# Two blocks on one core: the low halves of all weight chunks are subtracted on VectorE

## The chip, the cores and the metric

The program runs on one core of one Trainium2 chip. The metric is the device time of one execution in microseconds (us), the median over several runs. PE is TensorE's matmul part, PEld its weight load, DVE is VectorE, ACT is ScalarE, POOL is GpSimd, SP is SyncE, which here only issues DMAs.

## The reference, cut to what matters

The reference runs two transformer-like blocks over 512 tokens of width 1024, in fp32. The first has a recurrent branch (a short convolution and a gated linear recurrence) beside an attention branch; the second has a pooling branch, a differential attention branch over 512 latent and 256 context tokens, an RWKV branch (a recurrent state that is run forward and backward), a gated merge of the three, and a mixture of 32 experts. What touches the change are the large projections:

```
proj = einsum('bsd,de->bse', h, w_in[l])            # first block, 3072 columns
mix  = einsum('bse,ed->bsd', concat([ya, yb]), w_out[l])
p_l  = modulate(x, norm1_g, ...) @ w_in[l]          # second block, 7040 columns
p_c  = modulate(ctx, norm1_g, ...) @ w_in[l]        # the context's 256 tokens
merged = sum_n sigmoid(gates_n) * (branches[n] @ w_br[n]);  mix_l = merged @ w_out[l]
```

## The kernel before, in words

The tile framework assigns no engine: each instruction is written for one. Its planner then places all instructions of an engine in one order, by simulated costs of its own, and each engine executes its instructions strictly in that order; semaphores make them wait for one another.

Every projection is made with about fp32 accuracy out of three matmuls in a faster format (`mm3`, L307 to L312). For that each operand is split into a high part, which is the value rounded to that format, and a low part, which is the rest. The weights come from DRAM in chunks of 128 partitions x 1024 values (512 KB). `load_chunk` (L293) issues the DMA on SP, and `split_chunk` (L299) makes the two halves: ACT copies `raw` into `hi` (tile names `wr` and `wh` in the profile), and then `lo = raw - hi` (`wl`) is a TENSOR_TENSOR of 128x1024. Its engine is `cur.get("lo", GP)`: POOL, unless `cur["lo"]` has been set. There are 125 chunks. The first 50 belong to the first block and the context's projections, 53 to the RWKV stage of the second block (from L1089, where `cur["lo"] = V` is set, to L1520, where it is taken away), and 22 to what comes after: a few that the planner places beside the last RWKV batches, the three branch merges (`merge`, L1550) and the output projection (L1795).

The stages in order of time, in the traced execution: the first block's q, k, v projections, its attention, and its recurrent projections (0 to about 345 us, POOL makes `lo`); the first output projection and the context's projections, beside which the first block's result is normed (to 485 us, POOL); the RWKV stage (to about 1133 us, DVE); differential attention with the merges in between, and the output projection (to about 1440 us, POOL); the experts (to the end), whose weights are not split.

Names that the steps below touch: `rope` (L551; POOL makes `o = src*cos` at L554, DVE `a` at L556 and `o + a` at L559); `conv` (L931; `xa`); `tok_ss` (L1013; sums of squares, `sbs` on DVE at L1020, `sbp` on PE); `gate_b` (L1028; `yb` on POOL at L1032); `qk_norm` and L901 (the context's keys, `kc`); `rsq` (L320; a DVE step, then a power on POOL at L323, as in `rm`, `kcnr`, `h2r`); the scaling of the first block's result `mix` (L1070, L1073) and its norm (L426); `shift` (L724; tiles `al`, `kt`, `vt`, and a tile also called `wl`, L727 and L728, which is not the low half of weights); `scores` of the differential attention (L1652; `dpl` on PE, a maximum on DVE, `P` on ACT).

PE writes a projection's result into one of three PSUM buffers of the tag `mm`; a chunk's first matmul waits until the buffer that it takes has been read out.

Of the kernel before, what the change touches and what calls it, by code (L numbers as in the profile page):

```python
# [9 lines left out]
F32 = mybir.dt.float32  # L10
# [3 lines left out]
ALU = mybir.AluOpType  # L14
# [171 lines left out]
def build(tc, A, out, dbg=None, upto=99):  # L186
    with ExitStack() as ctx:
        _build(ctx, tc, A, out, dbg, upto)


def _build(ctx, tc, A, out, dbg, upto):
    nc = tc.nc
    V, SC, GP, PE, SY = nc.vector, nc.scalar, nc.gpsimd, nc.tensor, nc.sync
# [5 lines left out]
    cur = {}  # L199

    def weights(name, bufs, side, raw=None):

        if cur.get("wctx"):
            cur["wctx"].close()
            cur["wctx"] = None
        if bufs:
            cur["wctx"] = ctx.enter_context(ExitStack())
            cur["wp"] = cur["wctx"].enter_context(tc.tile_pool(name=name, bufs=1, side=side, reuse_waits="tile"))
            cur["wb"] = bufs
            cur["wraw"] = raw or bufs  # L210
# [3 lines left out]
    def subpool(name, nb):  # L214

        if cur.get("sub"):
            cur["sub"].close()
            cur["sub"] = None
        if nb is None:
            return  # L220
        cur["sub"] = ctx.enter_context(ExitStack())
        cur["bp"] = cur["sub"].enter_context(tc.tile_pool(name=name, bufs=1, reuse_waits="tile"))
        NB.clear()
        NB.update(nb)
# [17 lines left out]
    def psum(name, bufs):  # L242

        if "pctx" in cur:
            cur["pctx"].close()
        cur["pctx"] = ctx.enter_context(ExitStack())
        cur["pp"] = cur["pctx"].enter_context(tc.tile_pool(name=name, bufs=1, space=PSUM, reuse_waits="tile"))
        PB.clear()
        PB.update(bufs)
# [43 lines left out]
    def load_chunk(w, c0, kt=8, name="w", nw=128, k0=0, kn=2):  # L293

        raw = cur["wp"].tile([128, kt, nw], F32, tag="raw", name=name + "r", bufs=cur["wraw"])
        n = c0 // 128 if nw == 128 else c0 // 256 * kn + k0 // 4
        cur["ld"] = SY.dma_start(raw.rearrange("p k n -> p (k n)"), w[n]).ins
        return raw

    def split_chunk(raw, name="w"):  # L300
        kt, nw = raw.shape[1], raw.shape[2]
        hi = cur["wp"].tile([128, kt, nw], F32R, tag="hi", name=name + "h", bufs=cur["wb"])
        lo = cur["wp"].tile([128, kt, nw], F32R, tag="lo", name=name + "l", bufs=cur["wb"])
        SC.activation(hi, raw, AF.Copy)  # L304
        cur.get("lo", GP).tensor_tensor(lo, raw, hi.bitcast(F32), ALU.subtract)  # L305
        return hi, lo

    def mm3(p, ah, al, bh, bl, start, stop):
# [42 lines left out]
    def step(n=1):  # L351

        while n and fill:
            try:
                next(fill[0])
                n -= 1
            except StopIteration:
                fill.pop(0)
# [158 lines left out]
    def halves(w, c0):  # L517

        return [split_chunk(load_chunk(w, c0, kt=4, nw=256, k0=4 * kh)) for kh in range(2)]
# [566 lines left out]
    weights(None, 0, None)  # L1086
    cp2 = wctx.enter_context(tc.tile_pool(name="c2", bufs=1, side="right", reuse_waits="tile"))
    weights("wp1", 3, "right", 2)
    cur["lo"] = V  # L1089
    psum("pp2", {"mm": (2, 512), "aux": (3, 512), "ch": (1, 512), "pa": (2, 512)})  # L1090
    scope("b2a", {})
    rp = cur["bp"]
# [425 lines left out]

    gate(24 - GL - ngate[0])
    step(99)  # L1520
    cur.pop("lo")
    subpool(None, None)


# [264 lines left out]
    for c in range(4):  # L1789
        po2 = [ps("po2", "aux" if c % 2 else "mm") for _ in range(2)]  # L1790
        for kh in range(2):
            hi, lo = split_chunk(load_chunk(A["w_out_2"], 256 * c, kt=4, nw=256, k0=4 * kh))
# [339 lines left out]
```

## Time and profile before

| | us |
|---|---|
| runs shown | 1940.88, 1953.85, 1959.17 |
| median | 1953.85 |
| the profiled execution's own time | 1948.57 |
| its span, first to last instruction | 1946.8 |

| engine | busy us | share of the span |
|---|---|---|
| PE | 1732.8 | 89% |
| DVE | 1062.6 | 55% |
| ACT | 618.2 | 32% |
| POOL | 406.4 | 21% |

Of POOL's 406.4 us the 72 subtractions of weight chunks are 181.3. The mean granted TensorE clock is 0.938 of full speed, and it switches between two levels, 1.2 and 2.4 GHz. Busy time is that of instructions from start to end; an instruction of DVE or POOL that cannot go on is counted as busy too.

### The profile page before, as it was taken

The page shows a single profiled execution, that of the slowest core. Times are in us where ns is not written, and L with a number is a line of the kernel's source. Part 1 is how long each engine was busy: PE and PEld are TensorE (multiplying, and loading weights), DVE is VectorE, ACT ScalarE, POOL GpSimd, SP SyncE. Part 2 cuts the span into 40 slices and gives each one's busy share as a digit, 9 for nine tenths or more (in the row PEclk, how much of TensorE's full clock was granted, in tenths as well). Part 3 has the DMA queues.
Part 4 walks back from the last instruction along what each step waited for, and adds up shares of the span by engine and source line. Part 5 has one row for each costly group of instructions (what it writes and reads, how often), then busy time and mean ns, then how long its engine had stood idle before and what let it go on. Part 6 is the DMA issues. An engine that isn't in the chain of part 4 may idle for free.

```text
span 1946.8 us, 31337 instructions
## 1 busy us (share of the span) xinstructions
PE 1732.8 (89%) x12309; PEld 1233.5 (63%) x12310; DVE 1062.6 (55%) x2417; ACT 618.2 (32%) x1164; POOL 406.4 (21%) x326
## 2 busy tenths in 40 slices
PE   6899997966888988978889986989979999999998
PEld 3874567963565777767768864777944545444544
DVE  4555686174479845767777744676342333332432
ACT  4224454453444232333333333443221111110110
POOL 2520337351004101111220013722211010100000
PEclk8999998988988997889989998989989999999999
DMA  8335622567647545445565346635449999999998
GB/s 294 108 112 207 215 76 90 171 217 223 173 128 194 148 141 115 138 93 142 140 147 144 108 160 210 234 122 177 186 165 386 386 386 386 386 387 387 386 386 288
DMA packets 275296, 415.90 MB, mean 214 GB/s; under 512 B 104876, under 2 KB 126408, under 8 KB 274888
## 3 DMA queue, kind: packets, MB, share of 16 engines
q1 hardware_dynamic: 246248, 383.44, 59.4%
q10 hardware_dynamic: 25568, 16.78, 2.8%
q0 software_dynamic: 3328, 13.63, 2.5%
q8 instruction: 98, 1.61, 0.3%
q14 instruction: 54, 0.44, 0.1%
HBM read 370.26 MB, written 43.53 MB: 213 GB/s over the span
## 4 chain that ended last, share of the span: by engine, by line
PE 43%; DVE 5%; DMA 5%; ACT 1%; issue 1%; SPq 0%; POOL 0%; ACTq 0%; DVEq 0%; POOLq 0%
PE ped L1976 6%; PE peg L1937 6%; PE peu L1944 6%; PE pcb L2008 3%; PE po L1799 2%; PE pg L1910 2%; DMA kb<-kbD 2%; PE pg L1911 2%; PE pW L1283 1%; PE pf L312 1%; PE pf L310 1%; PE pf L311 1%; PE pbr L310 1%; PE pbr L311 1%; PE pbr L312 1%; PE dpo L1683 1%
## 5 line engine op out<-in xcount | busy, mean ns | idle before, releaser
L305 POOL TENSOR_TENSOR wl<-wr,wh 128x1024 fp32r<-128x1024 f32 x72 | 181.3, 2528 | 306.6 <-ACT wh L304 300.2
L304 ACT ACTIVATE wh<-wr 128x1024 fp32r<-128x1024 f32 x125 | 131.7, 1055 | 172.7 <-PE pf L311 61.0
L310 PE MATMUL pf<-h2h,wh 128*128 128x512 f32 x344 | 144.5, 420 | 20.7 <-ACT mth L1348 14.4
L311 PE MATMUL pf<-h2l,wh 128*128 128x512 f32 x344 | 142.6, 415 | 0.0
L312 PE MATMUL pf<-h2h,wl 128*128 128x512 f32 x344 | 141.8, 412 | 0.0
L1982 POOL TENSOR_TENSOR yl<-ey,yh 128x512 fp32r<-128x512 f32 x30 | 38.4, 1280 | 464.6 <-ACT yh L1981 464.6
L1976 PE MATMUL ped<-wd,hid 128*64 128x512 f32 (+1 forms) x528 | 127.4, 585 | 0.7 <-ACT hid L1960 0.7
L1937 PE MATMUL peg<-wg,hTg 128*64 128x512 f32 x512 | 127.0, 597 | 0.0
L1944 PE MATMUL peu<-wu,hTg 128*64 128x512 f32 x512 | 125.2, 595 | 0.0
L1195 DVE TENSOR_TENSOR Tm<-LT,Ti 128x60 f32<-128x60 f32 (+24 forms) x372 | 87.5, 235 | 43.2 <-DMA LT<-atD 35.0
L2009 DVE TENSOR_TENSOR acc<-acc,pcb 128x512 f32<-128x512 f32 (+1 forms) x124 | 76.0, 665 | 49.1 <-PE pcb L2008 49.0
L310 PEld LDWEIGHTS pf<-h2h,wh 128*128 128x128 f32 x344 | 67.5, 196 | 40.7 <-ACT mth L1348 14.7
L1197 DVE TENSOR_TENSOR Ti<-Ti,Tm 128x60 f32<-128x60 f32 (+24 forms) x372 | 82.4, 221 | 8.4
L1976 PEld LDWEIGHTS ped<-wd,hid 128*64 128x64 f32 x528 | 39.6, 136 | 70.9 <-issue 67.1
L1944 PEld LDWEIGHTS peu<-wu,hTg 128*64 128x64 f32 x512 | 42.9, 137 | 65.4 <-issue 64.1
L305 DVE TENSOR_TENSOR wl<-wr,wh 128x1024 fp32r<-128x1024 f32 x53 | 65.1, 1228 | 32.3 <-ACT wh L304 32.0
L1937 PEld LDWEIGHTS peg<-wg,hTg 128*64 128x64 f32 x512 | 41.9, 137 | 60.9 <-issue 58.4
L311 PEld LDWEIGHTS pf<-h2l,wh 128*128 128x128 f32 x344 | 67.6, 196 | 18.1 <-issue 3.2
L312 PEld LDWEIGHTS pf<-h2h,wl 128*128 128x128 f32 x344 | 67.2, 195 | 17.4 <-issue 1.1
L1981 ACT ACTIVATE yh<-ey 128x512 fp32r<-128x512 f32 x30 | 18.9, 630 | 163.5 <-DVE ey L1980 90.0
L1914 ACT ACTIVATE hTg<-pg,sh,gs 128x128 f32<-128x128 f32 x64 | 28.2, 457 | 121.4 <-PE peu L1944 55.4
L1917 DVE TENSOR_SCALAR hTg<-pg,gs,sh 128x128 f32<-128x128 f32 x64 | 25.3, 408 | 75.0 <-PE peu L1944 38.4
(962 smaller groups left out, 4468.0 us busy)
## 6 DMA issues: line engine op xcount, KB each, us to landing
wg<-in_w_exp_gate_dram SPq DMA_DIRECT2D x64, 1024.0 KB
wu<-in_w_exp_up_dram SPq DMA_DIRECT2D x64, 1024.0 KB
wd<-in_w_exp_down_dram SPq DMA_DIRECT2D x62, 1024.0 KB
wr<-in_w_in_dram SPq DMA_DIRECT2D x97, 512.0 KB
kb<-kbD SPq DMA_DIRECT2D x24, 384.0 KB
wr<-in_w_out_dram SPq DMA_DIRECT2D x16, 512.0 KB
LT<-atD SPq DMA_DIRECT2D x12, 512.0 KB
thD<-mth ACTq DMA_DIRECT2D x24, 256.0 KB
```

The costliest lines, as they stand in the source:

```text
L304: SC.activation(hi, raw, AF.Copy)
L305: cur.get("lo", GP).tensor_tensor(lo, raw, hi.bitcast(F32), ALU.subtract)
L310: PE.matmul(p, ah, bh, start=start, stop=False)
L311: PE.matmul(p, ah, bl, start=False, stop=False)
L312: PE.matmul(p, al, bh, start=False, stop=stop)
L1195: V.tensor_tensor(tmp[:, :nj, :n], bc(LT[:, s, None, ts_], [128, nj, n]), bc(T[:, js, s:s + 1], [128, nj, n]), ALU.mult)
L1197: V.tensor_tensor(T[:, js, ts_], T[:, js, ts_], tmp[:, :nj, :n], ALU.add)
L1937: mm = PE.matmul(pg[64 * a:64 * a + 64, :], hT[:, k, 64 * a:64 * a + 64], gp[a][k // 4][:, k % 4, :], start=(k == 0), stop=(k == 7), tile_ ...
L1944: PE.matmul(pu[64 * a:64 * a + 64, :], hT[:, k, 64 * a:64 * a + 64], up[a][k // 4][:, k % 4, :], start=(k == 0), stop=(k == 7), tile_posit ...
L1976: PE.matmul(pd[64 * a:64 * a + 64, :], hid[:, m * k + 64 * a:m * k + 64 * a + 64], dn[q][a][:, k, 0:q1 - q0], start=(k == 0), stop=(k == 3 ...
L2008: PE.matmul(p, ohT[R, 128 * i:128 * (i + 1)], yy[R, qs], start=(z == 0), stop=(z == len(parts) - 1))
L2009: V.tensor_tensor(acc[i][:, qs], acc[i][:, qs], p, ALU.add)
```

## The change

`split_chunk` subtracts on VectorE always, and the two lines that switched the engine around the RWKV stage are gone.

```diff
@@ split_chunk
         SC.activation(hi, raw, AF.Copy)
-        cur.get("lo", GP).tensor_tensor(lo, raw, hi.bitcast(F32), ALU.subtract)
+        V.tensor_tensor(lo, raw, hi.bitcast(F32), ALU.subtract)
         return hi, lo
@@ before the RWKV stage
     weights("wp1", 3, "right", 2)
-    cur["lo"] = V
@@ after it
     step(99)
-    cur.pop("lo")
     subpool(None, None)
```

The planner makes a new order from it. All 125 subtractions stand on DVE, and none on POOL. The order of the first half of the RWKV stage is what it was; in its second half chunks and batches are interleaved otherwise.

On POOL, around the gating of the first block's attention branch, before (`yb` is the gated branch, `sar`, `sbr` and `kcnr` are powers in `rsq`):

```order
L305 TENSOR_TENSOR wl<-wr,wh 128x1024 x14
L1032 TENSOR_TENSOR yb_1457<-yb_1457,gbth 128x512
L305 TENSOR_TENSOR wl<-wr,wh 128x1024
L1032 TENSOR_TENSOR yb_1672<-yb_1672,gbth 128x512
L323 TENSOR_TENSOR sar<-sar,cst_75 128x4
L305 TENSOR_TENSOR wl<-wr,wh 128x1024
L1032 TENSOR_TENSOR yb_1911<-yb_1911,gbth 128x512
L305 TENSOR_TENSOR wl<-wr,wh 128x1024
L1032 TENSOR_TENSOR yb_2101<-yb_2101,gbth 128x512
L305 TENSOR_TENSOR wl<-wr,wh 128x1024 x2
L323 TENSOR_TENSOR sbr<-sbr,cst_75 128x4
```

and on POOL at the same place now:

```order
L1032 TENSOR_TENSOR yb_1457<-yb_1457,gbth 128x512
L1032 TENSOR_TENSOR yb_1672<-yb_1672,gbth 128x512
L1032 TENSOR_TENSOR yb_1911<-yb_1911,gbth 128x512
L323 TENSOR_TENSOR sar<-sar,cst_75 128x4
L1032 TENSOR_TENSOR yb_2101<-yb_2101,gbth 128x512
L323 TENSOR_TENSOR sbr<-sbr,cst_75 128x4
L323 TENSOR_TENSOR kcnr<-kcnr,cst_75 128x8 x2
```

Nothing stands between the gating steps any more.

On DVE, at the rotary embedding of q (`qra` and `qro` are `a` and `o` of `rope`, `xc` is the context), before:

```order
L556 TENSOR_TENSOR qra<-q_377,SIN 128x512
L426 TENSOR_SCALAR xc_2127<-xc_2127,hcr 128x1024
L426 TENSOR_SCALAR xc_2129<-xc_2129,hcr 128x1024
L556 TENSOR_TENSOR qra<-q_378,SIN 128x512
L559 TENSOR_TENSOR qro<-qro,qra 128x512
L556 TENSOR_TENSOR qra<-q_379,SIN 128x512
L559 TENSOR_TENSOR qro<-qro,qra 128x512 x2
L556 TENSOR_TENSOR qra<-q_380,SIN 128x512
L559 TENSOR_TENSOR qro<-qro,qra 128x512
```

and on DVE at the same place now:

```order
L426 TENSOR_SCALAR xc_2127<-xc_2127,hcr 128x1024
L426 TENSOR_SCALAR xc_2129<-xc_2129,hcr 128x1024
L305 TENSOR_TENSOR wl<-wr,wh 128x1024 x2
L556 TENSOR_TENSOR qra<-q_377,SIN 128x512
L559 TENSOR_TENSOR qro<-qro,qra 128x512
L556 TENSOR_TENSOR qra<-q_378,SIN 128x512
L559 TENSOR_TENSOR qro<-qro,qra 128x512
L556 TENSOR_TENSOR qra<-q_379,SIN 128x512
L559 TENSOR_TENSOR qro<-qro,qra 128x512
L305 TENSOR_TENSOR wl<-wr,wh 128x1024
L556 TENSOR_TENSOR qra<-q_380,SIN 128x512
L305 TENSOR_TENSOR wl<-wr,wh 128x1024
```

Four subtractions have come in, one of them between the last two steps of the rotation (the last `qro` follows the last row).

On DVE, where the first block's result is scaled beside the context's projections (`pf` is a projection in PSUM, `mix` the first block's result), before:

```order
L322 TENSOR_SCALAR rm<-ssm 128x4
L727 SCALAR_TENSOR_TENSOR wl<-pf,vec,wl 128x255
L728 SCALAR_TENSOR_TENSOR wl<-pf,vec,wl 128x255
L1070 SCALAR_TENSOR_TENSOR mix_3173<-mix_3173,rm,gpb 128x1024
...
L727 SCALAR_TENSOR_TENSOR al<-pf,vec,al 128x255
L1073 TENSOR_TENSOR mix_3173<-x_0_3673,mix_3173 128x1024
L1073 TENSOR_TENSOR mix_3174<-x_1_3678,mix_3174 128x1024
L728 SCALAR_TENSOR_TENSOR al<-pf,vec,al 128x255
L727 SCALAR_TENSOR_TENSOR kt<-pf,vec,kt 128x255
```

and on DVE at the same place now:

```order
L1070 SCALAR_TENSOR_TENSOR mix_3176<-mix_3176,rm,gpb 128x1024
L727 SCALAR_TENSOR_TENSOR wl<-pf,vec,wl 128x255
L305 TENSOR_TENSOR wl<-wr,wh 128x1024
L727 SCALAR_TENSOR_TENSOR al<-pf,vec,al 128x255
L1073 TENSOR_TENSOR mix_3173<-x_0_3673,mix_3173 128x1024
L1073 TENSOR_TENSOR mix_3174<-x_1_3678,mix_3174 128x1024
L305 TENSOR_TENSOR wl<-wr,wh 128x1024
L728 SCALAR_TENSOR_TENSOR wl<-pf,vec,wl 128x255
L728 SCALAR_TENSOR_TENSOR al<-pf,vec,al 128x255
...
L426 TENSOR_SCALAR mix_3176<-mix_3176,h2r 128x1024
L305 TENSOR_TENSOR wl<-wr,wh 128x1024
L727 SCALAR_TENSOR_TENSOR kt<-pf,vec,kt 128x255
```

The read-out of the first two projections (L727, L728) has moved behind the scaling, and that of `kt` behind the norm of the result (L426).

## Rows read from the trace of the kernel before

**Rows 1.** Busy time by stage: us, busy us (instructions) of each engine, clock, DMA.
```profile
0.00:485.00 485.00, 413.75 (x2784) 313.23 (x2785) 268.39 (x462) 210.92 (x410) 167.65 (x88) 0.93 0.51 171
745.00:1133.00 388.00, 342.95 (x3913) 295.40 (x3912) 281.46 (x912) 131.26 (x261) 54.00 (x82) 0.93 0.52 131
1133.00:1440.00 307.00, 257.96 (x1565) 216.15 (x1564) 174.06 (x300) 113.73 (x216) 106.37 (x69) 0.92 0.50 174
1440.00:1946.80 506.80, 493.34 (x2588) 239.65 (x2586) 163.68 (x309) 64.82 (x123) 38.39 (x30) 1.00 1.01 373
```
**Rows 2.** Line L305: ns shortest/median/longest, first to last start; then who waited (us, times).
```profile
L305 POOL TENSOR_TENSOR wl<-wr,wh x72: 2346/2407/3382, 38.8 to 1397.3; 128x1024 fp32r<-128x1024 f32 x72
L305 DVE TENSOR_TENSOR wl<-wr,wh x53: 1199/1220/1709, 485.5 to 1133.0; 128x1024 fp32r<-128x1024 f32 x53
...
  ACT wh L304: 19.2, 8
  PEld pf L312: 0.8, 1
```
**Rows 3.** Waits of PE in 0 to 100 us: us, times, longest.
```profile
PE qTT L568 <- DVE qro L559: 5.2, 3, 2.7
PE pt L312 <- DVE h1l L444: 2.3, 2, 1.4
```
**Rows 4.** Waits of PE in 100 to 300 us.
```profile
PE pr L973 <- DVE xa L940: 3.0, 2, 2.8
```
**Rows 5.** Waits of PE in 300 to 485 us.
```profile
PE pf L310 <- DVE al L728: 7.3, 1, 7.3
PE h2T L435 <- DVE mix L426: 5.9, 2, 4.6
PE sbp L1023 <- DVE sbs L1020: 4.5, 1, 4.5
PE kcTT L568 <- DVE kc L901: 3.1, 1, 3.1
```
**Rows 6.** Waits of PE in 1240 to 1420 us.
```profile
PE dpl L1657 <- ACT P L1660: 9.0, 5, 4.1
```
**Rows 7.** Waits of PE in 1100 to 1240 us.
```profile
PE pm L1610 <- POOL gy L1608: 18.7, 1, 18.7
```
**Rows 8.** DVE in order of time, 388 to 440 us: start, us, line, shape, count.
```profile
395.15 13.30 DVE L1070 SCALAR_TENSOR_TENSOR mix<-mix,rm,gpb 128x1024 f32<-128x1024 f32 x4 [0.91 <-POOL rm L323]
...
412.33 1.22 DVE L1073 TENSOR_TENSOR mix<-x,mix 128x1024 f32<-128x1024 f32 x1
```
**Rows 9.** POOL in order of time, 388 to 440 us.
```profile
395.06 12.31 POOL L305 TENSOR_TENSOR wl<-wr,wh 128x1024 fp32r<-128x1024 f32 x4
```
**Rows 10.** DVE in order of time, 296 to 318 us.
```profile
295.43 0.68 DVE L1020 TENSOR_TENSOR sas<-sas,saq 128x512 f32<-128x512 f32 x1
...
305.27 0.48 DVE L1043 TENSOR_SCALAR yb<-yb,vec 128x512 f32<-128x512 f32 x1
305.70 2.85 DVE L1020 TENSOR_TENSOR sbs<-sbs,sbq 128x512 f32<-128x512 f32 x1
308.48 4.06 DVE L1043 TENSOR_SCALAR yb<-yb,vec 128x512 f32<-128x512 f32 x2
312.46 3.63 DVE L1020 TENSOR_TENSOR sbs<-sbs,sbq 128x512 f32<-128x512 f32 x2
```
**Rows 11.** DVE in order of time, 54 to 100 us.
```profile
73.41 4.50 DVE L559 TENSOR_TENSOR qro<-qro,qra 128x512 f32<-128x512 f32 x2
...
78.61 0.69 DVE L559 TENSOR_TENSOR qro<-qro,qra 128x512 f32<-128x512 f32 x1
```
**Rows 12.** DVE in order of time, 244 to 256 us.
```profile
246.48 4.29 DVE L940 SCALAR_TENSOR_TENSOR xa<-xraw,vec,xa 128x509 f32<-128x509 f32 x3
...
251.26 2.32 DVE L940 SCALAR_TENSOR_TENSOR xa<-xraw,vec,xa 128x509 f32<-128x509 f32 x3
```
**Rows 13.** Busy time in two stretches, columns as in Rows 1.
```profile
77.10:83.90 6.80, 5.94 (x28) 5.94 (x29) 2.10 (x3) 0.38 (x1) 0.26 (x1) 0.50 0.22 77
316.00:322.90 6.90, 6.75 (x31) 6.75 (x32) 6.14 (x13) 3.14 (x6) 4.44 (x2) 0.51 0.17 63
```
**Rows 14.** The chain that ended last, in order of time: start, us, what.
```profile
851.83 13.24 DMA kb<-kbD
```

## What is predicted, before the change has run

> **What bounds the kernel now.** I read the busy time by stage first [rows 1]. In the last stage, the experts, the DMA share is 1.01 and PE is busy 493.34 of 506.80 us: nothing here is touched, and it keeps its length. In the three earlier stages PE is the busiest engine everywhere, with 413.75 of 485, 342.95 of 388 and 257.96 of 307 us, so that time can come only out of its waits and out of stretches at the lower clock. Neither DVE nor POOL is near full in a stage: DVE has 268.39 of 485 us in the first. Whether PE ever waits for the subtraction itself is told by its line [rows 2]: of all 125, on either engine, PE's weight load waited for one, 0.8 us, and ACT eight times, 19.2 us in all, for a buffer that POOL still read. So POOL's 2407 ns against DVE's 1220 ns per chunk is by itself worth nothing. Then I read PE's own waits in the stages where POOL subtracts [rows 3 to 6]. Nearly all of the long ones are waits for DVE, on steps that have nothing to do with weights. Last, I looked at DVE in time at those places, and there the price of the old arrangement shows.
>
> **What POOL's subtraction does to DVE.** At 395.15 four DVE steps on 128x1024 take 13.30 us; a step of the same size with no POOL work beside it takes 1.22 us, so four need 4.9, and 8.4 us are lost [rows 8]. In exactly that stretch POOL makes four `wl` in 12.31 us, 3.1 each instead of 2.4 [rows 9]: the two engines take turns. At 305.70 the same shows with short steps: a `sbs` takes 2.85 us where a `sas` of the same size takes 0.68, two `yb` take 4.06 where one takes 0.48, two more `sbs` take 3.63; together 10.54 us instead of 3.0, 7.5 lost [rows 10]. Two `qro` take 4.50 us, and one alone 0.69: 3.1 lost [rows 11]. Three `xa` take 4.29 us, and the next three 2.32: 2.0 lost [rows 12]. So at four places alone 21 us of DVE's "busy" time is standing still for POOL.
>
> **What the change adds and removes.** 72 subtractions leave POOL (72 x 2.5 us) and cost DVE 72 x 1.22 = 88 us, 61 of them in the first 485 us, where DVE then has at most 268 + 61 = 329 of 485 us, and the rest after 1133 us. Against this stand the lost times above, 21 us at the places shown; from above they are bounded by POOL's whole time on the 72. The DMAs are the same, and the expert stage has no such subtraction.
>
> That the added work delays no weights is read from the RWKV stage, where DVE already makes all 53 and no wait of PE names one [rows 2]; so for a subtraction queued behind other DVE steps I take 2 us in all (below 0; above, all 88 us less the 21 shown, 67, if DVE set PE's pace everywhere, which its share of the stages excludes).
>
> Now wait by wait, each with zero and its full length as bounds:
>
> - `h1l`, 2.3 us [rows 3]: four subtractions, 4.9 us, now stand among the eight `h1l`, about what their turns with POOL cost them. I take 1.
> - `qro`, 5.2 us [rows 3]: DVE loses 3.1 here, and POOL's own half of the rotation no longer stands behind two subtractions, but one subtraction (1.22) now stands before the last `qro`. I take 4.
> - `xa`, 3.0 us [rows 4]: 2.0 are lost to the lock. I take 2.
> - `sbs`, 4.5 us [rows 5]: 7.5 are lost, more than the wait, and POOL's gating steps are not interleaved with subtractions any more; at most 1.22 comes in between. I take 4.5.
> - `kc`, 3.1 us [rows 5]: its power on POOL and its two DVE steps were in turn with subtractions. I take 3.
> - `al`, 7.3 us [rows 5]: 8.4 us of lock go, but two subtractions (2.4 us) now stand among the steps before the read-out of both projections is done, and PE has some small matmuls left to do afterwards that it did during the old wait. I take 4.
> - `P`, 9.0 us [rows 6]: chains of the differential attention that alternate PE, DVE, ACT; POOL's `wl` holds a step of them now and then. DVE gets these subtractions as well. I take 2.
>
> Sum 20.5 us. The stall of 18.7 us on `gy` is a DMA's round trip behind the RWKV stage [rows 7]: no part of it goes.
>
> The clock: right behind the `qro` and the `sbs` wait the granted clock fell to 0.50 and 0.51, the lower of its two levels, with PE busy 5.94 and 6.75 us there [rows 13]. At the upper level that work takes half: 6.3 us in the two stretches if both waits go. I take 5, since PE may still pause a little there; below 0.
>
> Against it: in the new order the read-out of `kt` stands behind the norm of the first block's result. Before, PE lost 5.9 us to that norm later [rows 5]; bounds are 0 and these 5.9 once more, and I take 3. The second half of the RWKV stage is interleaved anew with the same work: its sign can't be read from an order, so I take 0, with 8 us (2% of 388, the part of PE's idle time there that an order can move) to both sides.
>
> Sum: 20.5 + 5 - 2 - 3 = 20.5 us less. From the profiled execution's own 1948.6 us that gives **1928 us**. The median of the runs stood 5 us above that execution, so against a median the same saving reads about 1933; I keep to the execution's scale.
>
> **The rivals.**
>
> *Nothing is won.* DVE gets 88 us of real work in place of the time it stood locked; at the places shown the lock is 21 us. If the chains that PE waits for have as much new work in front of them as they lost in lock, the waits stay: 1949 us, plus or minus 8. For it speaks the new order on DVE, where subtractions stand in the middle of those very chains; against it that the lock came at every step of a chain, and the subtraction comes once (7.5 us against 1.22 at `sbs`). The Trainium skill, Perfetto Trace Analysis, Optimizing Scalar/DVE Operations, says that because GpSimd and VectorE share a read port of SBUF, moving work between these two might not help. By that the time would be this rival's; the trace speaks for the shared port, and against the conclusion, since POOL's instruction is twice as long as DVE's [rows 2] and holds others up meanwhile. Chance 0.22.
>
> *The RWKV stage gets slower.* The chain that ended last passes there through loads of `kb`, one of which alone is 13.24 us [rows 14], and these are issued on SP in an order that has changed from the middle of the stage on. Of the eight batches in that half (n = 4 to 11), three with one more such load bare on the path would cost 3 x 13.24 = 39.7 us: 1928 + 40 = 1968 us. It decides from two on (26.5 us, more than the whole gain); the lower bound is one, which leaves the change within 1%. For it: SP's order moved more there than anywhere. Against it: the batches follow each other as before, and the loads are still issued about one batch ahead. Chance 0.12.
>
> *Everything comes back.* All waits named above go entirely: 2.3 + 5.2 + 3.0 + 4.5 + 3.1 + 7.3 + 9.0 = 34.4 us, and 6.3 of clock, 40.7 in all, with the 5.9 of `mix` to spare for the new places: 1908 us, and with a lucky RWKV order a little less. For it: the locks lie in front of all of them. Against it: waits for a chain seldom vanish whole. Chance 0.16.
>
> That the change doesn't do what it says is out: POOL has no such subtraction left in the order.
>
> **How the numbers follow.** The forecast (1928, its own range 1917 to 1940) has 0.50. About 1%, 19.5 us, is what a measurement of this kernel tells from no change: the bound lies at 1929, almost at the forecast. Faster by more: two thirds of the forecast's chance, since its terms were taken short where a lock was larger than its wait, 0.33, and the whole of the last rival, 0.16: 0.49. Slower by more: the RWKV rival, 0.12. Within 1%: the rest, 0.39. The range 1903 to 1955 takes in the last rival with a few us of luck, the forecast and the first rival with most of its spread, and leaves out the RWKV rival and the tails.
>
> **What would show it.** In the changed kernel's profile: L305 on DVE 125 times at about 1.22 us, 153 us in all, and no POOL row; the four `mix` steps near 4.9 us instead of 13.30; `sbs` near 0.68 each; the waits on `sbs`, `kc` and `qro` gone from PE's list, and the first stage shorter than 485 us by some 15 to 20 us; no wait of PE for `wl` above 2 us. The forecast is wrong if DVE's steps stay long with POOL idle, if PE's list shows new waits for `wl` or for `kt`, or if the stretch from 745 to 1133 us changes by more than 8 us.

## The result, and the profile after

The changed kernel takes 1922.78 us (median, 1918.96 to 1932.67), the kernel before 1956.51 us beside it (1940.88 to 1959.26; the three runs of the table before, and a fourth). The ratio is 0.9843, with a 95% interval of 0.9803 to 0.9883: faster by more than 1%. The profiled execution takes 1923.72 us with a span of 1921.9, against 1948.57 and 1946.8: 24.9 us less, where 20.5 were forecast (1928).

Where they went is read from PE's marks, the first matmul of a kind in each trace (`pt` is the first projection, `ps` the attention, `sap` the first gating sum, `pa` the output projection, `pA` the RWKV stage, `pm` the stage behind it, `prk` the router):

| from ... to | before, us | after, us | gained | forecast |
|---|---|---|---|---|
| start to `pt` | 41.1 | 41.0 | 0.1 | 0 |
| `pt` to `ps` | 73.1 | 67.5 | 5.6 | 7.5 (`h1l` 1, `qro` 4, half the clock's 5) |
| `ps` to `sap` | 182.0 | 179.0 | 3.0 | 2 (`xa`) |
| `sap` to `pa` | 47.5 | 35.1 | 12.4 | 10 (`sbs` 4.5, `kc` 3, half the clock's 5) |
| `pa` to `pA` | 151.3 | 153.1 | -1.8 | 1 (`al` 4, `kt` -3) |
| `pA` to `pm` | 685.1 | 682.2 | 2.9 | 0 plus or minus 8 |
| `pm` to `prk` | 246.2 | 243.1 | 3.1 | 2 (`P`) |
| `prk` to the end | 520.5 | 520.9 | -0.4 | 0 |

The 2 us taken off for late `wl` had no place of their own. The new order puts 17 matmuls more in front of the first `sap` (1032 from `ps` to `sap`, before 1015), about 2 us of work by their pace of 28 in 3 us, so the third row gained some 2 us more and the fourth some 2 us less than the table says. (Line numbers of the changed kernel are one less than before's behind L1089 and two less behind L1520; the experiments shift them by a few lines too.)

Busy time in the changed kernel, columns as in [rows 1]: the first 485 us, and the stretch from `sap` to `pa`:

```profile
0.00:485.00 485.00, 426.97 (x2868) 323.45 (x2870) 272.99 (x539) 223.90 (x430) 45.49 (x45) 0.94 0.55 179
287.50:322.60 35.10, 28.73 (x227) 27.33 (x226) 25.54 (x43) 19.65 (x34) 10.79 (x6) 1.00 0.41 130
```

and from `sap` to `pa` in the kernel before:

```profile
296.20:343.70 47.50, 38.28 (x242) 36.38 (x243) 29.23 (x36) 21.41 (x36) 36.30 (x18) 0.86 0.31 99
```

DVE is the column to look at (the third busy time). In the first 485 us it has 539 instructions instead of 462, among them the 50 subtractions of the first part and the first steps of the RWKV stage, which begins 19 us earlier, and yet its busy time goes from 268.39 only to 272.99 us. Over the whole span it goes from 1062.6 to 1067.5 us, with 72 x 1.22 = 88 us of work added: about 83 us in which DVE was counted as busy and stood still have gone. In the stretch from `sap` to `pa` the clock column goes from 0.86 to 1.00; PE is busy there for 28.73 instead of 38.28 us, with 227 instead of 242 instructions in the window.

The subtraction's line in the changed kernel, in ns as in [rows 2]:

```profile
L305 DVE TENSOR_TENSOR wl<-wr,wh x125: 1199/1222/1915, 38.8 to 1372.3; 128x1024 fp32r<-128x1024 f32 x125
...
  PEld pf L312: 1.2, 2
```

The granted clock fell five times between `pt` and `pa` before, each time right behind a wait of PE (for `qro`, `xa`, `sbs`, `kc` and ACT's `vc`), and falls once now. The five stretches before (columns as in [rows 1]):

```profile
77.10:83.93 6.83, 5.97 (x28) 5.97 (x29) 2.10 (x3) 0.38 (x1) 0.26 (x1) 0.50 0.22 77
251.18:254.60 3.42, 3.42 (x8) 2.08 (x7) 3.28 (x6) 0.00 (x0) 0.00 (x0) 0.50 0.27 105
316.04:322.86 6.82, 6.71 (x31) 6.71 (x32) 6.10 (x13) 3.14 (x6) 4.40 (x2) 0.50 0.17 63
329.69:333.10 3.41, 3.41 (x17) 3.41 (x18) 1.59 (x4) 0.81 (x1) 1.64 (x1) 0.50 0.49 159
339.93:343.34 3.41, 3.41 (x18) 3.41 (x17) 0.00 (x0) 1.06 (x1) 0.45 (x1) 0.50 0.44 108
```

and the one now, at a new wait of PE for ACT's `q`:

```profile
55.18:62.01 6.83, 5.68 (x26) 5.68 (x27) 2.81 (x4) 3.89 (x9) 0.70 (x1) 0.50 0.18 53
```

DVE in order of time, at the rotation, the gating and the scaling that [rows 8, 10, 11] show before:

```profile
77.50 0.68 DVE L559 TENSOR_TENSOR qro<-qro,qra 128x512 f32<-128x512 f32 x1
...
293.95 1.78 DVE L1020 TENSOR_TENSOR sbs<-sbs,sbq 128x512 f32<-128x512 f32 x1
...
296.45 0.68 DVE L1020 TENSOR_TENSOR sbs<-sbs,sbq 128x512 f32<-128x512 f32 x1
...
298.19 0.68 DVE L1020 TENSOR_TENSOR sbs<-sbs,sbq 128x512 f32<-128x512 f32 x1
...
373.63 4.87 DVE L1070 SCALAR_TENSOR_TENSOR mix<-mix,rm,gpb 128x1024 f32<-128x1024 f32 x4
```

The four scaling steps take 4.87 instead of 13.30 us, two of three `sbs` 0.68. The first `sbs` still takes 1.78: POOL's gating step `yb`, which reads two tensors too, runs beside it (293.72 to 295.19 us).

PE's waits after, in the windows 0 to 100, 287 to 323, 368 to 476, 1090 to 1230 and 1230 to 1400 us:

```profile
PE pt L310 <- ACT q L546: 3.9, 1, 3.9
PE pt L312 <- DVE h1l L444: 0.5, 1, 0.5
...
PE kcTT L568 <- DVE kc L901: 2.1, 2, 1.6
PE pt L310 <- ACT kc L546: 2.0, 1, 2.0
...
PE pf L310 <- DVE wl L728: 7.4, 1, 7.4
PE pf L310 <- DVE kt L728: 6.5, 2, 4.5
PE pf L310 <- ACT wh L304: 3.2, 1, 3.2
...
PE pm L1608 <- POOL gy L1606: 14.0, 1, 14.0
...
PE dpl L1655 <- ACT P L1658: 9.2, 3, 4.3
```

Beside [rows 3 to 7]: the waits for `qro`, `xa`, `sbs` and the norm's `mix` are gone; the one for `kc` has lost only 1.0 us, with a new one of 2.0 for ACT's `kc` beside it; that of `al` is there again under the name of `wl`, as long as before; the one for `kt` has grown from 1.2 to 6.5; `P` has not moved; `gy` has become shorter.

### The profile page after: what moved, and what is told of

It is laid out like the page before. It is cut to its first block, busy times and chain, and to the rows that moved or that the text cites. A ratio compares the mean times of both kernels' runs of the same rounds, so it can differ in the third digit from the quotient of the medians.

```text
span 1921.9 us, 31334 instructions
## 1 busy us (share of the span) xinstructions
PE 1723.0 (90%) x12309; PEld 1227.1 (64%) x12310; DVE 1067.5 (56%) x2489; ACT 620.5 (32%) x1166; POOL 226.2 (12%) x254
## 4 chain that ended last, share of the span: by engine, by line
PE 67%; DMA 14%; DVE 11%; ACT 3%; issue 3%; SPq 1%; POOL 1%; ACTq 0%; DVEq 0%; POOLq 0%
PE ped L1974 6%; PE peu L1942 6%; PE peg L1935 6%; PE pf L310 4%; PE pf L312 4%; PE pf L311 4%; DMA kb<-kbD 4%; PE pcb L2006 3%; DMA LT<-atD 3%; PE po L1797 2%; PE pW L1282 2%; PE pg L1908 2%; PE pt L310 2%; PE pt L312 2%; PE pt L311 2%
## 5 line engine op out<-in xcount | busy, mean ns | idle before, releaser
L305 DVE TENSOR_TENSOR wl<-wr,wh 128x1024 fp32r<-128x1024 f32 x125 | 154.0, 1232 | 62.8 <-ACT wh L304 61.2
L310 PE MATMUL pf<-h2h,wh 128*128 128x512 f32 x344 | 144.4, 420 | 19.2 <-ACT mth L1347 15.6
L1942 PEld LDWEIGHTS peu<-wu,hTg 128*64 128x64 f32 x512 | 43.3, 137 | 67.5 <-issue 64.4
L310 PE MATMUL pt<-wh,h1h 128*128 128x256 f32 x192 | 56.6, 297 | 6.6 <-ACT q L546 3.9
```

The lines of the kernel that those rows point to most:

```text
L305: V.tensor_tensor(lo, raw, hi.bitcast(F32), ALU.subtract)
L310: PE.matmul(p, ah, bh, start=start, stop=False)
L1942: PE.matmul(pu[64 * a:64 * a + 64, :], hT[:, k, 64 * a:64 * a + 64], up[a][k // 4][:, k % 4, :], start=(k == 0), stop=(k == 7), tile_posit ...
```

## The experiments

Theory A: POOL's subtraction makes VectorE stand still, and that is what was won. Rivals: POOL's own steps of a chain came late behind 2.4 us pieces of work (B); the planner's new order did it (C); and, about the price, whether the subtractions that VectorE got instead are free (D, J, K). For kernels with an extra or a missing step in the first part, the length from `pt` to `pA` is the measure, each time from one traced execution: the first part's code is the same in the changed kernel and in two others, and they have 434.7, 435.3 and 433.6 us there; it is the same in the kernel before and in the second experiment, and they have 453.9 and 451.8. So 2 us say nothing there. The whole time is a worse measure, as will be seen.

**One part alone.** The first 50 subtractions on VectorE, the last 22 on POOL:

```diff
     psum("pp", {"mm": (3, 512), "aux": (3, 512), "big": (2, 512)})
+    cur["lo"] = V
```

> The first 50 subtractions go to VectorE, the last 22 stay on POOL. Theory A (POOL's subtraction stops VectorE's steps, wherever both run): the 19.3 us that the changed kernel gained before the RWKV stage stay, and RWKV starts at about 476 us; the 5.6 us that it gained from there on go, and PE's wait for `gy` behind the RWKV stage is again about 18.7 us instead of 14.0. Ratio to the kernel before about 0.990. Rival C (the gain is the planner's new order as a whole): the split needn't follow the place of the subtractions; either part may lose or keep everything, 0.984 or 1.000.

Measured: 1928.66 us, ratio 0.9888 (0.9855 to 0.9921). `pt` to `pA` 435.3 us, as in the changed kernel; `pm` to `prk` 248.4 instead of 243.1. So the gain of the first part sits where the subtractions were taken from POOL, and in the second part the stretch with POOL's subtractions is longer again. One expectation failed: the wait for `gy` is 13.5 us, not 18.7, though POOL makes two subtractions in front of it.

The opposite, the last 22 alone:

```diff
     step(99)
-    cur.pop("lo")
```

> Only the last 22 subtractions go to VectorE, the first 50 stay on POOL. Theory A: the first 485 us are those of before (RWKV starts at 495 us), and some 5 us are gained behind the RWKV stage, nearly all of them at `gy`, whose wait falls from 18.7 to about 14, since POOL issues the loads of the attention heads some 25 us earlier when no subtraction stands in front of them. Ratio 0.997. Rival C (order): anything from 0.99 to 1.00 with the wait for `gy` unchanged.

Measured: 1947.32 us, ratio 0.9967 (0.9944 to 0.9991). `pt` to `pA` 451.8 us against 453.9 before; the wait for `gy` is 13.7. Ratio and wait are as expected, but the gain is not where it was expected: from `pA` to the end this trace has 1453.2 us against 1451.8 before (`pm` to `prk` 245.9 against 246.1), and what it gains lies in front of `pA`, where its code is that of before. So the 5 us of the last 22 subtractions are not shown.

**POOL busy again, in three ways.** The changed kernel, with useless work for POOL behind each of the first 50 subtractions. First the same subtraction:

```diff
         V.tensor_tensor(lo, raw, hi.bitcast(F32), ALU.subtract)
+        if not cur.get("rw"):          # set where the RWKV stage begins
+            GP.tensor_tensor(raw, raw, hi.bitcast(F32), ALU.subtract)
```

> The changed kernel, but behind each of the first 50 subtractions on VectorE POOL makes the same subtraction once more, in place on the raw chunk, which nobody reads afterwards. Theory A (POOL's reading stops VectorE) and rival B (POOL's own steps of a chain come late behind 2.4 us pieces of work) both expect the gain before the RWKV stage gone: RWKV starts at 490 to 505 us instead of 476, ratio 0.994 to 1.005, and the four scaling steps on 128x1024 take about 13 us again instead of 4.9. Rival C (the planner's order, or the shorter latency of the subtraction): RWKV still starts at about 476 to 480 us, ratio 0.984 to 0.987.

Measured: 1983.57 us, ratio 1.0173 (1.0140 to 1.0205). RWKV starts at 529.8 us, `pt` to `pA` is 489.2: worse than either theory had it, and worse than before, since VectorE has its own 50 subtractions besides, and they and POOL's stop each other (VectorE's `wl` takes 1452 ns on average over all 125 instead of 1232). DVE and POOL at the scaling:

```profile
429.25 9.07 DVE L1072 SCALAR_TENSOR_TENSOR mix<-mix,rm,gpb 128x1024 f32<-128x1024 f32 x4 [0.51 <-POOL rm L325]
```
```profile
429.19 5.66 POOL L307 TENSOR_TENSOR wr<-wr,wh 128x1024 f32<-128x1024 f32 x2
```

Two POOL steps, 5.66 us, and VectorE loses 9.07 - 4.87 = 4.2 us beside them. An order alone (C) stretches no step, and RWKV did not start at 476 to 480 us. The useless steps also hold the raw chunks longer, which could make weights late; but PE waits for `wh` 5.0 us up to `pA` here and 3.2 in the changed kernel, and its long waits are for VectorE again (`kt` 10.4, `kc` 8.9, `sbs` 5.6, `al` 5.2, `h1l` 4.5, `xa` 4.2).

Then fillings with constants, which read nothing:

```diff
+        if not cur.get("rw"):
+            GP.memset(raw, 0.0)
+            GP.memset(raw, 0.0)
+            GP.memset(raw[:, :kt // 2], 0.0)
```

> The changed kernel, but behind each of the first 50 subtractions POOL overwrites the raw chunk, which nobody reads afterwards, with constants: two of 128x1024 and one of 128x512, about 2.4 us together as one subtraction took, and reading nothing. Theory A (it is POOL's reading that stops VectorE): RWKV starts at 476 to 482 us, the four scaling steps stay near 4.9 us, ratio 0.984 to 0.988. Rival B (POOL's time in its queue delays its own steps): RWKV starts at 488 to 500 us with the scaling steps near 4.9 us, ratio 0.992 to 1.00. If writing alone also stops VectorE: scaling steps at 8 to 13 us.

Measured: 1950.87 us, ratio 0.9990 (0.9967 to 1.0014), RWKV starts at 485.3 us. By the whole time Theory A would have fallen; the trace says where its expectation went wrong. DVE and POOL at the scaling:

```profile
384.17 4.87 DVE L1074 SCALAR_TENSOR_TENSOR mix<-mix,rm,gpb 128x1024 f32<-128x1024 f32 x4 [0.51 <-POOL rm L327]
```
```profile
384.55 0.95 POOL L308 MEMSET wr<- 128x1024 f32 x1
...
387.81 0.52 POOL L309 MEMSET wr<- 128x512 f32 x1
```

POOL is at work nearly through the whole scaling, and VectorE takes the 4.87 us that it takes alone. Of VectorE's two-input steps on 128x1024 in the first 500 us, 31 overlap such fillings by a tenth of their length or more; 30 of them take under 1.3 us, and the mean is 1263 ns. In the experiment before 27 overlap the useless subtractions, 8 take under 1.3 us, and the mean is 2432 ns. The Trainium skill, SBUF — State Buffer, Who interferes with whom, says that such a step contends with a POOL instruction that reads SBUF and not with one that only writes it; both rows agree.

But the fillings don't leave all of VectorE alone. Its steps with one tensor as input meet them and are stretched. The first step of each `xa` of the convolution, 128x512, beside the fillings:

```profile
L941 DVE TENSOR_SCALAR xa<-xraw,vec x4: 1087/1253/1374, 229.1 to 247.7; 128x512 f32<-128x512 f32 x4
```

and in the changed kernel:

```profile
L937 DVE TENSOR_SCALAR xa<-xraw,vec x4: 539/540/543, 225.2 to 241.4; 128x512 f32<-128x512 f32 x4
```

Summed step by step up to `pA`, VectorE's TENSOR_SCALAR steps take 16.0 us more than in the changed kernel, its two-input steps 1.3. So the fillings are a control for the two-input steps alone.

The rest of the time went elsewhere, twice. From the first to the last `ps` the same 574 matmuls take 94.2 us instead of 86.4, because the granted clock is at the lower level for some 17 us in the middle of the attention, with no wait of PE (columns as in [rows 1]):

```profile
133.00:136.00 3.00, 3.00 (x15) 1.87 (x15) 0.74 (x3) 0.49 (x2) 0.00 (x0) 0.95 0.78 294
136.00:139.00 3.00, 3.00 (x11) 1.08 (x11) 0.94 (x3) 0.60 (x2) 0.00 (x0) 0.50 0.03 11
...
151.00:154.00 3.00, 3.00 (x16) 0.74 (x13) 0.00 (x0) 0.66 (x2) 0.00 (x0) 0.71 0.85 273
```

The experiment before has the same stretch (94.2 us), the others don't; its cause is open. `pt` to `pA` is 445.9 us here and was 489.2 with the subtraction, against 434.7 in the changed kernel. With the 7.8 us of clock taken off both, the fillings cost 3.4 us and the subtraction 46.7: POOL's time in its own queue (B), with the stretched one-input steps, is the small part, its reading of two tensors the large one. And `pA` to `prk`, whose code is that of the changed kernel, takes 944.1 instead of 925.3 us; the planner's order is another there, of which more below.

Then a step that reads one tensor instead of two:

```diff
+        if not cur.get("rw"):
+            GP.tensor_scalar(raw, raw, 1.0, None, op0=ALU.mult)
```

> The changed kernel, but behind each of the first 50 subtractions POOL multiplies the raw chunk, which nobody reads afterwards, by one in place: a step of the same size that reads one tensor instead of two. Filling with constants left VectorE's steps alone (four scaling steps in 4.87 us), a second subtraction on POOL stopped them. If one tensor read by POOL stops VectorE too: two-input steps of VectorE that meet it are stretched, POOL's own step as well, and RWKV starts at 485 us or later. If only two tensors do: VectorE's durations stay as in the changed kernel, RWKV starts at 475 to 480 us (484 to 488 if TensorE's clock falls in the attention, as it did for 16 us with the constants).

Measured: 1927.79 us, ratio 0.9872 (0.9826 to 0.9917), RWKV starts at 475.4 us, `pt` to `pA` 435.9 us. Neither expectation holds as it stands: the start is that of the second, but VectorE's durations do not stay. DVE and POOL at the scaling:

```profile
384.49 6.43 DVE L1072 SCALAR_TENSOR_TENSOR mix<-mix,rm,gpb 128x1024 f32<-128x1024 f32 x4
```
```profile
380.92 9.46 POOL L307 TENSOR_SCALAR wr<-wr 128x1024 f32<-128x1024 f32 x3
```

VectorE's four steps run within three steps of POOL and lose 1.6 us, not the whole of them. Of its two-input steps on 128x1024, counted as above, 37 overlap such a POOL step; 26 take under 1.3 us, and the mean is 1430 ns. The same section of the Trainium skill, SBUF — State Buffer, Who interferes with whom, calls the contention an exclusive lock; with one tensor read by POOL most of these steps are not held up at all here, and the measurement decides. The waits for `kc` (5.0) and `sbs` (2.8) came back, and shorter stretches elsewhere paid for them (`pt` to `ps` 64.1 instead of 67.5 us, `pa` to `pA` 148.9 instead of 153.1). This speaks against B once more: such a step takes POOL longer than a subtraction (2.80 us in the middle instead of 2.41), and `pt` to `pA` is only 1.2 us longer than in the changed kernel.

**What VectorE's new work costs.** The subtraction on VectorE twice:

```diff
+        if not cur.get("rw"):
+            V.tensor_tensor(raw, raw, hi.bitcast(F32), ALU.subtract)
```

> The changed kernel, but VectorE makes each of the first 50 subtractions a second time, in place on the raw chunk, which nobody reads afterwards: 50 x 1.22 = 61 us more work for VectorE before the RWKV stage, none for POOL. Theory A (what was won is VectorE's standing still, and the subtractions that it got instead cost next to nothing): RWKV starts at 476 to 483 us, as in the changed kernel (475.7). Rival D (the subtractions delay the chains that PE waits for by about what the standing still did, so that the gain hides a loss of like size): RWKV starts at 490 us or later, the waits for `sbs`, `kc` and `qro` are back with 2 us and more each. The whole time is read with care, since the order of the second half of the RWKV stage is made anew by any change.

Measured: 1952.64 us, ratio 1.0005 (0.9984 to 1.0026), RWKV starts at 499.1 us, `pt` to `pA` 457.7 us. Theory A's "next to nothing" falls and Rival D holds: 61 us more for VectorE, which was busy 272.99 of the first 485 us, cost 23.0 us, and the three waits are back (`qro` 3.2 us; the other two from 290 to 345 us):

```profile
PE kcTT L570 <- DVE kc L903: 7.3, 2, 4.5
PE sbp L1025 <- DVE sbs L1022: 3.6, 1, 3.6
```

Then none at all:

```diff
+        if not cur.get("rw"):
+            return hi, hi
         V.tensor_tensor(lo, raw, hi.bitcast(F32), ALU.subtract)
```

> The changed kernel without the first 50 subtractions on any engine: the three matmuls take the high half in place of the low one, so this part is computed less accurately, and no engine has that work; all else, PE's work too, is the same. A second set of these 61 us on VectorE made RWKV start 23.4 us later (499.1 against 475.7). Theory J (the first set costs as much as the second: the change pays some 20 us for the subtractions and wins some 40 us by POOL's silence): RWKV starts at 450 to 458 us. Rival K (the first 61 us fit into VectorE's idle time, as the prediction took with 2 us, and only the second set is too much): RWKV starts at 471 to 477 us.

Measured: RWKV starts at 461.7 us, between the two expectations; `pt` to `pA` 422.3 us. So the first 50 subtractions cost 453.9 - 422.3 = 31.6 us on POOL and 434.7 - 422.3 = 12.4 us on VectorE; the second set costs 23.0. The gain of the first part, 19.2 us, is the difference of two prices, each known to some 2 us. Part of both is clock: from `pt` to `pA` the clock is at the lower level for 63.4 us before, 48.3 in the changed kernel and 35.9 here. The whole time is 1920.88 us, ratio 0.9836 (0.9790 to 0.9883), not different from the changed kernel's: `pA` to `prk` took 939.2 instead of 925.3 us.

**The wait that stayed.** The read-out of two projections ahead of the scaling:

```diff
-    NC = (2, 0, 99)
+    NC = (2, 2, 99)
...
-        V.scalar_tensor_tensor(dstt[:, :n - 1], ...
+        sh = V.scalar_tensor_tensor(dstt[:, :n - 1], ...
+        cur["sh"] = sh.ins
...
+        with tc.issue_after(cur["sh"]):
             V.scalar_tensor_tensor(mix[i], mix[i], rm[:, i:i + 1], GPB, ...)
```

> The changed kernel, but the four scaling steps of the first block's result are put behind the read-out of the context's first two projections (`wl` and `al`), which in the changed kernel stand behind them on VectorE. Theory E (the wait of 7.4 us for the read-out of `wl` is made by the order alone: the scaling and three subtractions, 8.5 us, stand in front): that wait falls below 2 us, the one for `kt` (6.5 us) falls too since that read-out moves ahead of the norm, and the stretch from the end of the output projection to the RWKV stage (107.4 us) gets 4 to 8 us shorter; RWKV starts at 468 to 472 us. Rival F (PE has only the work behind those projections left, so that it waits for the norm instead): the wait moves to the transposes of the normed result, `h2T`, and RWKV starts at 474 to 478 us.

(`NC` says how many steps of the context's projections are written in front of each of three places in the program, `issue_after` holds an instruction behind another one.) Measured: 1923.49 us, ratio 0.9871 (0.9832 to 0.9911). RWKV starts at 469.2 us; from the end of the output projection to it 101.1 instead of 107.4 us. Theory E: the 7.4 us for `wl` are gone, made by the order. The part on `kt` failed (PE's waits from 368 to 470 us):

```profile
PE pf L310 <- DVE kt L728: 8.1, 3, 4.9
```

**The wait for `gy`.** POOL's row of the heads' loads and SP's of the results behind which they run, before:

```profile
1150.89 2.39 POOL L305 TENSOR_TENSOR wl<-wr,wh 128x1024 fp32r<-128x1024 f32 x1 [7.25 <-ACT wh L304]
1153.23 0.67 POOL L1585 DMA_DIRECT2D qs<-QS  x1
```
```profile
1159.56 2.93 SPq L1317 DMA_DIRECT2D yD<-yt  x2
```

and after:

```profile
1126.32 0.67 POOL L1583 DMA_DIRECT2D qs<-QS  x1 [12.80 <-ACT XW L1272]
```
```profile
1140.74 3.74 SPq L1316 DMA_DIRECT2D yD<-yt  x2
```

Before, 4 MB of loads are issued 6.3 us ahead of the results' write, now 14.4 us ahead. The test delays them:

```diff
         PE.matmul(pm, plw[:, g, :], dd, start=True, stop=True)
+        if g == 3:
+            for _ in range(36):
+                cur["hm"] = GP.memset(dd, 0.0).ins
...
-    head(0)
+    with tc.issue_after(cur["hm"]):
+        head(0)
```

> The changed kernel, but POOL issues the loads of the first two attention heads (4 MB) behind 36 useless fillings of 128x512 with constants, 18.7 us, and so about when the RWKV stage's last results are written instead of 15 us earlier. Theory H (the wait for `gy` behind the RWKV stage was shortened from 18.7 to 14.0 us because these loads no longer run beside the write and the reading back of `gy`): that wait is 17 to 22 us. Rival I (it was shortened by something else that the new order brought): it stays at 13.5 to 14.5 us.

Measured: 1922.43 us, ratio 0.9855 (0.9809 to 0.9901). POOL, and PE's wait:

```profile
1125.49 20.89 POOL L1513 MEMSET pld<- 128x512 f32 x36 [21.02 <-PE plm L1510]
1146.32 0.67 POOL L1586 DMA_DIRECT2D qs<-QS  x1
```
```profile
PE pm L1612 <- POOL gy L1610: 18.1, 1, 18.1
```

The wait is long again, but not by what Theory H says. The loads came too late, 14.6 us behind the write (at 1131.70), and POOL, which makes `gy` itself, got to it only behind them in its own queue:

```profile
1149.07 0.59 POOL L1586 DMA_DIRECT2D kl<-KL  x1
1149.62 1.33 POOL L1610 TENSOR_TENSOR gy<-gy,gy 128x512 f32<-128x512 f32 x1
```

So the run is no proof of the transfers. For them speaks the view of the DMA queues around this wait (packets, MB, share of the engines): before, from 1155 to 1181 us, POOL's loads take nearly half of the engines' time,

```profile
q0 software_dynamic: 847, 4.13, 44.7%
```

and after, from 1138 to 1159 us, next to none:

```profile
q0 software_dynamic: 99, 0.51, 6.3%
```

What became shorter is the time until the results' write has landed, for which SP waits before it issues the second read of `gy`; before:

```profile
SPq L1604 <- DMA yD<-yt: 7.0, 1, 7.0
```

and after:

```profile
SPq L1602 <- DMA yD<-yt: 1.6, 1, 1.6
```

These 5.4 us cover the 4.7 us of `gy`. The two half experiments, whose loads are issued 11.3 and 19.1 us ahead of the write, have waits for `gy` of 13.5 and 13.7 us. In the first of them 0.88 MB of POOL's loads still move behind the write (1139.2 to 1158 us), and yet SP waits 1.4 us. That makes the transfers likely, not shown.

**The same idea further.** Four more POOL steps to VectorE:

```diff
-                GP.tensor_tensor(dn(tha), dn(tha), k[:, None]...
+                V.tensor_tensor(dn(tha), dn(tha), k[:, None]...
...
-        GP.tensor_tensor(AR[:, :, 0, :], ...
+        V.tensor_tensor(AR[:, :, 0, :], ...
...
-        GP.tensor_tensor(k0, k0, k1, ALU.add)
+        V.tensor_tensor(k0, k0, k1, ALU.add)
...
-                GP.tensor_tensor(o.rearrange("p (h r) -> p h r", r=64), ...
+                V.tensor_tensor(o.rearrange("p (h r) -> p h r", r=64), ...
```

> The changed kernel, with four more two-operand steps moved from POOL to VectorE, those of the RWKV stage and beside the context (`tha`, `AR`, `gk`, and the cosine half `dro` of the rotation). POOL has 47 us of them, and VectorE stands still beside them for 24.7 us in the changed kernel's trace (9.7 for `tha`, 6.6 for `dro`, 5.2 for `AR`, 3.2 for `gk`). Theory A, applied to the next steps: VectorE's standing still goes there too, and where it lies in front of PE (the triangular inverses, whose steps of 0.2 us are stretched to 2 us) some of it comes back: 5 to 12 us, ratio to before 0.978 to 0.981. Rival G (VectorE is busy 68% of this stage against 56% of the whole, and PE waits there for chains through ACT and DMA too): no gain or a loss within 8 us, ratio 0.982 to 0.988.

Measured: 1905.00 us, ratio 0.9766 (0.9727 to 0.9804), more than either expectation; `pA` to `prk` 909.7 instead of 925.3 us. The triangular inverse's steps in the changed kernel (busy us, mean ns):

```profile
L1194 DVE TENSOR_TENSOR Tm<-LT,Ti 128x60 f32<-128x60 f32 (+24 forms) x372 | 86.9, 234 | 52.7 <-DMA LT<-atD 44.6
```

and here:

```profile
L1194 DVE TENSOR_TENSOR Tm<-LT,Ti 128x60 f32<-128x60 f32 (+24 forms) x372 | 77.2, 208 | 38.2 <-DMA LT<-atD 30.1
```

In the RWKV stage, from `pA` to the last `pch`, DVE has 1404 instructions instead of 1357 and is busy 463.3 instead of 466.6 us. All its runs (1902.08 to 1910.49) lie below all of the changed kernel's. How much of it is VectorE's standing still is open: the inverse's steps lost 9.7 us, but VectorE also waited 14.5 us less for the loads of `LT` in front of them, and the order is another one. With the read-out moved as well:

> The two experiments together that shortened a stage: the read-out of the context's first two projections ahead of the scaling (6.5 us less up to the RWKV stage), and `tha`, `AR`, `gk` and `dro` on VectorE (16.6 us less within it). If the two add up: RWKV starts at 468 to 470 us, ratio to before 0.972 to 0.975, some 1897 us. If the order of the second half of the RWKV stage, made anew, takes it back (it spread over 8 us and more between the kernels so far): 1905 us or slower.

Measured: 1910.08 us, ratio 0.9782 (0.9751 to 0.9813). `pt` to `pA` is 429.4, but `pA` to `prk` 920.7 instead of 909.7. By its time this is the second expectation; whether the order took it back or this one execution was a long one isn't shown. And the steps behind the RWKV stage (`hl2` and the two on `gt` written for `V` instead of `GP`):

> As the kernel with `tha`, `AR`, `gk` and `dro` on VectorE (1905 us), and the two-operand steps behind the RWKV stage there too: the low halves of the branches (`hl2`) and the two steps on `gt`. POOL keeps only powers, copies, fills, the rotations of the first block, `yb`, the sum `gy` and the experts' low halves. The order up to the end of the RWKV stage is that of the 1905 us kernel, so the two can be compared from there on. VectorE stands still behind the RWKV stage for 6.2 us because of these steps. Theory A as far as a gain is to be had: the stretch from the first `pm` to the router (244.6 us) gets 2 to 6 us shorter, ratio to before 0.973 to 0.976. Rival K2 (what PE waits for there are chains through ACT, `P` above all, and not these steps): within 2 us of 244.6, ratio 0.976 to 0.978.

Measured: 1904.71 us, ratio 0.9733 (0.9711 to 0.9754). `pm` to `prk` is 243.7 us against 244.6: Rival K2 by the stretch, though the ratio lies in the other range, which shows again that the whole time is the worse measure. PE waits there for `P`, in this kernel

```profile
PE dpl L1655 <- ACT P L1658: 9.9, 5, 4.3
```

The best two kernels are equal by their medians, 1905.00 and 1904.71 us.

## Why the prediction was right, and where it was not

- **The mechanism** held: POOL's two-tensor step stops VectorE's two-input steps, and this was read from rows of before [rows 8 to 12]. The same steps of POOL made again bring the long steps back; fillings of like length don't. Summed step by step, all VectorE steps but the subtractions take 1016.1 us in the changed kernel and 1092.4 before. POOL's latency was rightly taken as worth nothing: PE and its weight load waited 1.9 us in all for a subtraction after.
- **`qro`, `xa`, `sbs`, `kc` and `h1l`:** gained 21.0 us from `pt` to `pa`, clock included, where 19.5 were forecast. Three of the waits went whole. `kc`, forecast with 3, lost 1.0, and ACT's `kc` took 2.0 in its place. In place of `qro`'s 5.2 us stands one of 3.9 us for ACT's `q`, which this stretch's first estimate, 7.5, had not seen; 5.6 came.
- **The clock** was mis-sized: 5 forecast, half behind each of two waits. From `pt` to `pa` the clock was at the lower level for 29.2 us before and for 10.7 after; half of the 18.5 us between, about 9 us, is what that is worth with PE busy nearly throughout. Hardly any of it came at the rotation, where the wait for ACT's `q` brings a low stretch of its own; some 7 us came from `sap` to `pa`, where the prediction had seen one low stretch of three. So the waits themselves gave about 12 us where 14.5 were forecast.
- **"2 us in all" for subtractions queued behind other VectorE steps** was meant for weights that come late, and as that it held (1.9 us). But the reasoning beside it, that VectorE's share of the stages leaves room, failed: a second set of 61 us cost 23.0 us. VectorE's own steps behind the subtractions pay; the first set's price is 12.4 us, and POOL's was 31.6. By the prediction's figures up to the RWKV stage, the named waits and the clock add up to 31.7 us, and what it left of them standing, with the 2 and the 3 that it took off, to 13.2. The two totals came out nearly as measured, though `al`, `kc`, `kt` and the clock each came otherwise and the norm's 5.9 us was in neither: in part that is luck.
- **`al`, 4 us:** nothing came, 7.4 for 7.3. The prediction had read from the order that the read-out now stands behind the scaling, and yet credited the lock's end there. The read-out experiment shows that in the changed kernel the order was the whole wait. **`kt`, -3:** the wait rose from 1.2 to 6.5 us while the norm's 5.9 went; the sign was right. By the prediction's own signs a new wait for `kt` meant that the forecast was wrong; it came, and the forecast, which had taken 3 us off for it, stood. The sign was too strict.
- **`gy`, "no part of it goes":** 4.7 us went, with POOL's loads of the heads issued earlier and out of its way (likely, not proven). The prediction took the wait for a DMA's bare round trip and did not look at which transfers run beside it.
- **`P`, 2 us:** the wait stayed (9.2 for 9.0). The stretch gained 3.1 us all the same. The first experiment, with POOL subtracting there, lost 5.3 again, but the second, with VectorE subtracting there, has 245.9 us against 246.1 before; so whether the subtractions carry it is open.
- **The RWKV stage, 0 plus or minus 8:** it came at 2.9 better to `pm`, `gy` included. The bound was too narrow. From `pA` to `prk` the kernels with untouched code there (the changed one, those with more or less work for POOL or VectorE in the first part, and the read-out) take 925.3, 929.8, 944.1, 930.6, 938.0, 939.2 and 927.7 us, one traced execution each. The planner's order is not all of this spread of 19 us: the last two, the kernel without subtractions and the read-out, have one and the same order there on every engine, and differ by 11.5 us, with the clock at the lower level for 171.9 and 147.1 us. So a single trace says of this stage no more than to some 12 us, and what an order alone is worth is open.
- **The rivals.** "Nothing is won" has its mechanism in the 12.4 us, its price was too high. "RWKV gets slower" did not come; the longest such stretch, 18.8 us more in the kernel with the fillings, is less than the 26.5 from which that rival decides. "Everything comes back" did not, for `al` and `P`. The Trainium skill, Perfetto Trace Analysis, Optimizing Scalar/DVE Operations, has it that moving work between these two engines might not help; here it helped twice, 0.9843 and 0.9766.

## What to carry to other kernels

An engine's busy time may contain another engine's work: compare one step's duration alone with its duration beside POOL before taking a share of busy time as load. The price of a moved step is that of its new place, not zero where an engine has idle time: measure it by doing the step twice, and by leaving it out. A control has to be checked on every kind of step that it meets: the fillings left two-input steps alone and stretched one-input steps. Where a planner orders the program, judge an experiment by the stretch that it touches; the rest moves, with the order and from one execution to the next, by more than most edits are worth.

## What the runs showed of the hardware

- POOL's step that reads two tensors of 128x1024 holds up VectorE's steps with two inputs, and is held up by them (four steps 13.30 us instead of 4.87, POOL's 3.1 each instead of 2.4). POOL's fillings leave such steps alone (4.87) and stretch VectorE's one-input steps (`xa`, 128x512, 1.25 us instead of 0.54). A POOL step that reads one tensor stretches some of VectorE's two-input steps (four in 6.43).
- The granted clock fell to 0.50 for about 17 us in the attention, with PE's records without a gap and without a wait, in two kernels of the same matmuls, and in the others it stayed at 1.00; it cost 7.8 us.
